# Rotary embedding on one core: four start-up requests on SyncE's queue (x row 0, sine, x row 1, cosine) in place of three (sine, x rows 0 and 1, cosine)

## The chip, the cores and the metric

One core of one Trainium2 chip runs the kernel. The metric is the device time of one execution in microseconds (us), the median of repeated runs. The kernel before took 316.51 us, the median of three runs between 316.38 and 316.61. A separate execution was recorded by the hardware profiler; all views and records quoted here are of that execution.

## What is computed

A rotary position embedding is applied to x of shape (8, 2048, 16, 64): batch, position, head, channel. Each position has a row of 32 cosines and 32 sines, which all batches and heads share.

```
x1 = x[..., :32]
x2 = x[..., 32:]
out1 = x1 * cos - x2 * sin
out2 = x1 * sin + x2 * cos
out = concatenate([out1, out2], axis=-1)
```

Input and output are float32, 67.1 MB each. The arithmetic is small beside moving that much in and out of HBM.

## The kernel before

**Layout.** The 2048 positions of a batch are laid over 128 partitions, 16 consecutive positions to a partition (J = 16). One "row" j of a partition is one position: 16 heads by 64 channels, 1024 values, 4 KB in float32. A batch is thus 128 partitions of 16 rows, 8.4 MB in HBM. In the core's memory x is kept as float16 in `buf`, which has five slots (NBUF = 5); batch b uses slot b mod 5. The transfers issued from GpSimd (POOL) convert between float32 in HBM and float16 in `buf` on their way.

**Start-up.** Transfers issued from SyncE (SP) do not convert. So the first two rows of batch 0 (JA = 2) are fetched by SP in float32 into a tile of their own, `head` (8 KB to a partition, 1 MB in all, lines 41 to 44). The sine table goes to `sin_f` (line 40) and the cosine table to `cos_f` (line 45), each 2 KB to a partition and 256 KB in all. SP issues these three at the start, and nothing else until the end of the kernel. ScalarE (ACT) then casts, in this order: sine to `sin_h` (line 104), minus sine to the other half of `sin_h` (line 105), `head` to rows 0 and 1 of `buf` slot 0 (line 106), cosine to `cos_h` (line 110).

**GpSimd's transfers.** All other loads and stores are issued by POOL, on one queue, in an order that `in_ring` fixes (loads at line 71, stores at line 81):

1. load of rows 2 to 15 of batch 0
2. load of batch 1
3. store of row 0 of batch 0
4. load of batches 2 and 3 as one transfer, then of batch 4
5. store of rows 1 to 15 of batch 0, stores of batches 1 and 2
6. load of batches 5 and 6 as one transfer, then of batch 7 (slots 0, 1 and 2 again)
7. store of batches 3 and 4, store of batches 5 and 6, two stores with rows 0 to 13 of batch 7

The third entry has to wait until the first two rows of batch 0 are finished, and the fourth is behind it in POOL's order.

**Compute.** `rotate(b, j0, j1)` is three VectorE (DVE) instructions: v = swapped halves of x times the signed sine (line 92), x = x times cosine (line 98), x = x + v (line 100). DVE runs rotate for rows 0 and 1 of batch 0, for rows 2 to 15 of batch 0, and then for batches 1 to 7. The first line 92 needs `sin_h` and the cast `head`; the first line 98 needs `cos_h` too.

**End.** The last two rows of batch 7 are cast back to float32 by ACT into `head` (line 134) and stored by SP (line 135), which waits until the store of rows 0 to 8 of batch 7 has landed.

Of the kernel before, what the change touches and what calls it, by code (L numbers as in the profile page):

```python
# [1 line left out]

# [4 lines left out]


@with_exitstack  # L10
def kernel(
    ctx: ExitStack,
    tc: tile.TileContext,
    x: bass.AP,
    cos: bass.AP,
    sin: bass.AP,
    out: bass.AP,
):
    nc = tc.nc
    f16 = mybir.dt.float16  # L20
    f32 = mybir.dt.float32

    B, S, H, D = x.shape
    Dh = D // 2
    P = nc.NUM_PARTITIONS
    J = S // P
    NBUF = 5

    const_pool = ctx.enter_context(tc.tile_pool(name="rope_const", bufs=1))
    io_pool = ctx.enter_context(tc.tile_pool(name="rope_io", bufs=1))  # L30
    tmp_pool = ctx.enter_context(tc.tile_pool(name="rope_tmp", bufs=1))

    JA = 2
    head = const_pool.tile([P, JA, H, D], f32)
    x0 = x[0].rearrange("(p j) h d -> p j (h d)", j=J)
    sin_f = const_pool.tile([P, J, Dh], f32)
    cos_f = const_pool.tile([P, J, Dh], f32)
    cos_h = const_pool.tile([P, J, Dh], f16)
    sin_h = const_pool.tile([P, J, D], f16)
    nc.sync.dma_start(out=sin_f, in_=sin.rearrange("(p j) d -> p j d", j=J))  # L40
    nc.sync.dma_start(  # L41
        out=head.rearrange("p j h d -> p (j h d)"),
        in_=x0[:, 0:JA, :].rearrange("p j f -> p (j f)"),
    )
    nc.sync.dma_start(out=cos_f, in_=cos.rearrange("(p j) d -> p j d", j=J))

    buf = io_pool.tile([P, NBUF, J, H, D], f16)

    ring = []

    def in_ring(dma):
        if ring:
            tc.add_manual_dep(
                dma.ins,
                ring[-1].ins.name,
                mybir.DependencyInfo(mybir.DependencyClass.NoSync, mybir.DependencyReason.DATA),
                reason="order of the ring",
            )
        ring.append(dma)
        return dma  # L60

    def load(b, n=1):
        k = b % NBUF
        if n == 1:
            j0 = JA if b == 0 else 0
            dst = buf[:, k, j0:J, :, :].rearrange("p j h d -> p (j h d)")
            src = x[b].rearrange("(p j) h d -> p j (h d)", j=J)[:, j0:J, :].rearrange("p j f -> p (j f)")
        else:
            dst = buf[:, k : k + n, :, :, :].rearrange("p b j h d -> p b (j h d)")
            src = x[b : b + n].rearrange("b (p j) h d -> p b (j h d)", j=J)  # L70
        in_ring(nc.gpsimd.dma_start(out=dst, in_=src))  # L71

    def store(b, n=1, j0=0, j1=J):
        k = b % NBUF
        if n == 1:
            src = buf[:, k, j0:j1, :, :].rearrange("p j h d -> p (j h d)")
            dst = out[b].rearrange("(p j) h d -> p j (h d)", j=J)[:, j0:j1, :].rearrange("p j f -> p (j f)")
        else:
            src = buf[:, k : k + n, :, :, :].rearrange("p b j h d -> p b (j h d)")
            dst = out[b : b + n].rearrange("b (p j) h d -> p b (j h d)", j=J)  # L80
        return in_ring(nc.gpsimd.dma_start(out=dst, in_=src))  # L81

    def rotate(b, j0=0, j1=J):
        v = tmp_pool.tile([P, J, H, D], f16)
        n = j1 - j0
        js = slice(j0, j1)
        xt = buf[:, b % NBUF, js, :, :]
        shape = [P, n, H, 2, Dh]
        sin_b = sin_h[:, js, :].rearrange("p j (e d) -> p j e d", e=2).unsqueeze(2).to_broadcast(shape)
        cos_b = cos_h[:, js, :].unsqueeze(2).to_broadcast([P, n, 2 * H, Dh])  # L90
        xe = xt.rearrange("p j h (e d) -> p j h e d", e=2)
        nc.vector.tensor_mul(  # L92
            out=v[:, js, :, :].rearrange("p j h (e d) -> p j h e d", e=2),
            in0=xe[:, :, :, ::-1, :],
            in1=sin_b,
        )
        xw = xt.rearrange("p j h (e d) -> p j (h e) d", d=Dh)
        nc.vector.tensor_mul(out=xw, in0=xw, in1=cos_b)  # L98
        xa = xt.rearrange("p j h d -> p (j h d)")
        nc.vector.tensor_add(out=xa, in0=xa, in1=v[:, js, :, :].rearrange("p j h d -> p (j h d)"))  # L100

    load(0)
    load(1)
    nc.scalar.copy(out=sin_h[:, :, Dh:D], in_=sin_f)  # L104
    nc.scalar.mul(out=sin_h[:, :, 0:Dh], in_=sin_f, mul=-1.0)  # L105
    nc.scalar.copy(  # L106
        out=buf[:, 0, 0:JA, :, :].rearrange("p j h d -> p (j h d)"),
        in_=head.rearrange("p j h d -> p (j h d)"),
    )
    nc.scalar.copy(out=cos_h, in_=cos_f)  # L110
    rotate(0, 0, JA)
    store(0, 1, 0, 1)
    load(2, 2)
    load(4)
    rotate(0, JA, J)
    store(0, 1, 1, J)
    rotate(1)
    store(1)
    rotate(2)
    store(2)  # L120
    load(5, 2)
    load(7)
    rotate(3)
    rotate(4)
    store(3, 2)
    rotate(5)
    rotate(6)
    store(5, 2)
    rotate(7)
    gate = store(7, 1, 0, 9)  # L130
    store(7, 1, 9, J - JA)
    last = buf[:, 7 % NBUF, J - JA : J, :, :].rearrange("p j h d -> p (j h d)")
    dst = out[B - 1].rearrange("(p j) h d -> p j (h d)", j=J)[:, J - JA : J, :].rearrange("p j f -> p (j f)")
    nc.scalar.copy(out=head.rearrange("p j h d -> p (j h d)"), in_=last)  # L134
    end = nc.sync.dma_start(out=dst, in_=head.rearrange("p j h d -> p (j h d)"))
    tc.add_manual_dep(
        end.ins,
        gate.ins.name,
        mybir.DependencyInfo(mybir.DependencyClass.Sync, mybir.DependencyReason.DATA),
        reason="the last rows go out behind this part",  # L140
    )


# [1 line left out]
_INS = ['x', 'cos', 'sin']  # L145
_OUTS = [((8, 2048, 16, 64), 'float32')]


# [23 lines left out]
```

## Time and profile before

| what | value |
|---|---|
| median of the runs | 316.51 us |
| profiled execution: span from first to last instruction | 314.8 us (314.836 in the trace) |
| median minus span (start and end of an execution, outside the span) | 1.7 us |
| DVE busy | 209.1 us, 66% of the span |
| ACT busy | 6.8 us |
| POOL busy | 8.6 us |
| mean traffic in HBM | 428 GB/s over the span |
| first SP request issued / first POOL request issued | 0.74 us / 1.24 us |
| sine, head, cosine: issue to landing | 2.7, 6.9, 24.4 us |

How to read it: an instruction that issues a transfer costs its engine half a microsecond or so; the transfer itself is carried by the core's 16 DMA engines, which serve the queues of SP and POOL together. The view of issues gives the time from the issue to the landing, which is when the instruction that waits may start. The trace also holds a record of every piece that a DMA engine moved, with its start, its duration, its size and its queue. For a load or a store of 128 partitions there are 128 such pieces, eight to each DMA engine, one partition's share each (below called a *piece*), and after them on each engine a 4-byte piece that signals completion (below called a *mark*). Sizes in these records are those at the destination. Their times are given here from the start of the span.

### The profile page before, as it was taken

To read this page: it belongs to the slowest core of one execution; us is meant where nothing else is said; L and a number is where in the kernel's file an instruction comes from. 1 tells how busy PE (TensorE), PEld (TensorE's weight loads), DVE (VectorE), ACT (ScalarE), POOL (GpSimd) and SP (SyncE) were. 2 spreads that over 40 slices of the span, in tenths; PEclk is the share of its full clock that TensorE was granted. 3 is DMA by queue.
4 is the path that set the end of the run, shared out by engine and by line. 5 is a ranking of instruction groups with operands and counts; after the bars stand their busy time and mean duration, and the time that the engine had idled before them with its cause. 6 is when DMAs were issued, how large, how long until landed. Compare 5 with 4: busy or idle time off the path is not lost.

```text
span 314.8 us, 115 instructions
## 1 busy us (share of the span) xinstructions
DVE 209.1 (66%) x27; ACT 6.8 (2%) x6; POOL 8.6 (3%) x18
## 2 busy tenths in 40 slices
DVE  0105999999499999999950000899999999910000
ACT  3200000000000000000000000000000000020000
POOL 1002000000000000000010000000000000010000
DMA  9899999999999899999999999999999999999998
GB/s 284 187 262 200 200 266 200 200 262 204 200 200 317 382 492 407 400 400 533 400 200 208 258 200 200 229 237 333 400 491 441 400 400 525 408 400 400 433 427 339
DMA packets 3104, 101.71 MB, mean 323 GB/s; under 512 B 288, under 2 KB 288, under 8 KB 672
## 3 DMA queue, kind: packets, MB, share of 16 engines
q0 software_dynamic: 2528, 99.09, 98.1%
q1 hardware_dynamic: 576, 2.62, 2.2%
HBM read 67.63 MB, written 67.11 MB: 428 GB/s over the span
## 4 chain that ended last, share of the span: by engine, by line
DVE 66%; another core or an unknown queue 13%; DMA 8%; ACT 1%; issue 0%; SPq 0%; DVEq 0%; ACTq 0%
DVE buf L98 22%; DVE buf L100 22%; DVE v L92 22%; DMA cos_f<-in_cos_dram 8%; ACT head L134 1%; ACT cos_h L110 0%; SPq L41 0%; SPq L40 0%; DVEq L92 0%; ACTq L134 0%
## 5 line engine op out<-in xcount | busy, mean ns | idle before, releaser
L92 DVE TENSOR_TENSOR v<-buf,sin_h 128x16384 f16<-128x16384 f16 (+2 forms) x9 | 69.7, 7744 | 51.4 <-DMA buf<-in_x_dram 41.2
L98 DVE TENSOR_TENSOR buf<-buf,cos_h 128x16384 f16<-128x16384 f16 (+2 forms) x9 | 69.7, 7744 | 15.8 <-ACT cos_h L110 15.5
L100 DVE TENSOR_TENSOR buf<-buf,v 128x16384 f16<-128x16384 f16 (+2 forms) x9 | 69.7, 7744 | 0.3
L81 POOL DMA_DIRECT2D out_dram<-buf x8 | 4.7, 586 | 219.4 <-DVE buf L100 219.4
L134 ACT CAST head<-buf 128x2048 f32<-128x2048 f16 x1 | 1.9, 1898 | 249.9 <-DVE buf L100 249.9
L71 POOL DMA_DIRECT2D buf<-in_x_dram x6 | 3.7, 628 | 49.7 <-DMA out_dram<-buf 48.9
L106 ACT CAST buf<-head 128x2048 f16<-128x2048 f32 x1 | 1.9, 1897 | 3.5 <-DMA head<-in_x_dram 3.5
L104 ACT ACT_TABLE_LOAD x1 | 1.3, 1283 | 0.7 <-PEq L156 0.7
L110 ACT CAST cos_h<-cos_f 128x512 f16<-128x512 f32 x1 | 0.6, 617 | 16.1 <-DMA cos_f<-in_cos_dram 16.1
L104 ACT CAST sin_h<-sin_f 128x512 f16<-128x512 f32 x1 | 0.6, 617 | 1.4 <-DMA sin_f<-in_sin_dram 1.4
L105 ACT ACTIVATE sin_h<-sin_f 128x512 f16<-128x512 f32 x1 | 0.6, 624 | 0.0
L156 POOL MEMSET const-float32-0.0<- 128x1 f32 x1 | 0.1, 100 | 0.2 <-issue 0.2
L156 POOL MEMSET const-bfloat16-1.0<- 128x1 bf16 x1 | 0.1, 103 | 0.0
L156 POOL MEMSET const-float32-1.0<- 128x1 f32 x1 | 0.1, 100 | 0.0
L156 POOL MEMSET const-uint8-127<- 128x1 uint8 x1 | 0.1, 100 | 0.0
## 6 DMA issues: line engine op xcount, KB each, us to landing
buf<-in_x_dram POOLq DMA_DIRECT2D x2, 8192.0 KB, 55.2
buf<-in_x_dram POOLq DMA_DIRECT2D x3, 4096.0 KB, 57.4
out_dram<-buf POOLq DMA_DIRECT2D x1, 7680.0 KB, 68.3
out_dram<-buf POOLq DMA_DIRECT2D x1, 4608.0 KB, 28.6
buf<-in_x_dram POOLq DMA_DIRECT2D x1, 3584.0 KB, 22.3
out_dram<-buf POOLq DMA_DIRECT2D x1, 2560.0 KB, 34.1
head<-in_x_dram SPq DMA_DIRECT2D x1, 1024.0 KB, 6.9
out_dram<-head SPq DMA_DIRECT2D x1, 1024.0 KB, 8.4
```

Source lines behind the costliest of these rows:

```text
L71: in_ring(nc.gpsimd.dma_start(out=dst, in_=src))
L81: return in_ring(nc.gpsimd.dma_start(out=dst, in_=src))
L92: nc.vector.tensor_mul(out=v[:, js, :, :].rearrange("p j h (e d) -> p j h e d", e=2), in0=xe[:, :, :, ::-1, :], in1=sin_b,)
L98: nc.vector.tensor_mul(out=xw, in0=xw, in1=cos_b)
L100: nc.vector.tensor_add(out=xa, in0=xa, in1=v[:, js, :, :].rearrange("p j h d -> p (j h d)"))
L104: nc.scalar.copy(out=sin_h[:, :, Dh:D], in_=sin_f)
L105: nc.scalar.mul(out=sin_h[:, :, 0:Dh], in_=sin_f, mul=-1.0)
L106: nc.scalar.copy(out=buf[:, 0, 0:JA, :, :].rearrange("p j h d -> p (j h d)"), in_=head.rearrange("p j h d -> p (j h d)"),)
L110: nc.scalar.copy(out=cos_h, in_=cos_f)
L134: nc.scalar.copy(out=head.rearrange("p j h d -> p (j h d)"), in_=last)
L156: nc = _bacc.Bacc("TRN2", target_bir_lowering=False, num_devices=1)
```

## The change

Only the start-up requests of SP change. The request for `head` is split by rows, its first half goes ahead of the sine table, its second half behind it. The cosine table stays last. Per partition the four requests carry 4 KB, 2 KB, 4 KB and 2 KB where the three carried 2 KB, 8 KB and 2 KB.

```
-    nc.sync.dma_start(out=sin_f, in_=sin.rearrange("(p j) d -> p j d", j=J))
-    nc.sync.dma_start(
-        out=head.rearrange("p j h d -> p (j h d)"),
-        in_=x0[:, 0:JA, :].rearrange("p j f -> p (j f)"),
-    )
+    nc.sync.dma_start(out=head[:, 0, :, :].rearrange("p h d -> p (h d)"), in_=x0[:, 0, :])
+    nc.sync.dma_start(out=sin_f, in_=sin.rearrange("(p j) d -> p j d", j=J))
+    nc.sync.dma_start(out=head[:, 1, :, :].rearrange("p h d -> p (h d)"), in_=x0[:, 1, :])
     nc.sync.dma_start(out=cos_f, in_=cos.rearrange("(p j) d -> p j d", j=J))
```

The instructions of DVE, ACT, POOL and TensorE are the same, in the same order; SP has one more issue. ACT's cast of `head` is still one instruction over both rows, so it waits for both halves. Lines behind the edit stand two lower in the changed kernel (line 98 becomes line 96).

## The prediction

> **What bounds the kernel now.** I read the page's head first, then the issues, the timeline of the first 60 us, the chain, and last the trace's records of single pieces.
>
> ```profile
> DVE 209.1 (66%) x27; ACT 6.8 (2%) x6; POOL 8.6 (3%) x18
> ...
> DMA  9899999999999899999999999999999999999998
> ...
> HBM read 67.63 MB, written 67.11 MB: 428 GB/s over the span
> ```
>
> DVE is busy for two thirds only, while the DMA row is full from the first slice to the last. The piece records say it more sharply: from 2.2 us to 310.7 us all 16 DMA engines serve one piece after the other without a gap. So the span is the DMA engines' work plus whatever time they stand still, and an edit costs time if it adds work to them or lets their queues run dry.
>
> ```profile
> buf<-in_x_dram POOLq DMA_DIRECT2D x1, 3584.0 KB, 22.3
> ...
> head<-in_x_dram SPq DMA_DIRECT2D x1, 1024.0 KB, 6.9
> ...
> out_dram<-buf POOLq DMA_DIRECT2D x1, 512.0 KB, 15.2
> sin_f<-in_sin_dram SPq DMA_DIRECT2D x1, 256.0 KB, 2.7
> cos_f<-in_cos_dram SPq DMA_DIRECT2D x1, 256.0 KB, 24.4
> ```
>
> The sine and the cosine table are equally large; one takes 2.7 us to land and the other 24.4. That is the row to explain. What follows from it is in the timeline:
>
> ```profile
> 1.24 1.21 POOL L71 DMA_DIRECT2D buf<-in_x_dram  x2 [0.80 <-PEq L167]
> 1.65 0.42 SPq L45 DMA_DIRECT2D cos_f<-in_cos_dram  x1
> ...
> 26.10 0.62 ACT L110 CAST cos_h<-cos_f 128x512 f16<-128x512 f32 x1 [16.09 <-DMA cos_f<-in_cos_dram]
> 26.75 1.23 DVE L98 TENSOR_TENSOR buf<-buf,cos_h 128x2048 f16<-128x2048 f16 x1 [15.48 <-ACT cos_h L110]
> ...
> 29.53 0.54 POOL L81 DMA_DIRECT2D out_dram<-buf  x1 [27.08 <-DVE buf L100]
> ```
>
> Until the cosine is there (26.08), DVE cannot finish rows 0 and 1, POOL cannot issue their store (29.53), and the loads of batches 2 to 4 stand behind that store. Meanwhile the DMA engines live on the two loads issued at 1.24. Their last mark is at 42.7 to 43.1 us in the piece records, and the store's pieces follow at once.
>
> **Why the cosine is late.** Each DMA engine carries 8 pieces and a mark of every request. From the records of one engine: sine pieces 0.084 us each, head pieces 0.309 us, first load 2.13 us, second load 2.43 us. Sine and head are served in one run from 1.8 to 5.3-5.6 us. Then come a piece of the load, the mark of head, a piece of the load, a cosine piece, a piece of the load, a cosine piece, and so on: cosine pieces begin at about 9.7, 11.8, 14, 16.2, 18.4, 20.6, 22.8 and 23.1 us, the marks at 25.4-25.7. So **one piece of SP's queue is served for each entry of POOL's queue.** Of SP's 27 entries, 17 or 18 went ahead and 9 or 10 were left to alternate; the tenth turn ends at 25.7, which gives the landing.
>
> The question that decides this case is what put the border behind the eighth head piece. All 16 engines have it there, though they reach it between 5.28 and 5.62 us, so a software load that became ready at one moment near 5.4 us would have found them at different pieces. The end of the kernel shows another mechanism.
>
> ```profile
> 305.57 0.35 SPq L135 DMA_DIRECT2D out_dram<-head  x1
> ```
>
> SP's first piece at the start began 1.03 us after its issue (0.74 to 1.77). Here it begins at 310.72, 5.2 us after the issue: on every engine five pieces of POOL's store that had not begun by 306.6 (0.79 us each) and its mark still go first. They were **already in a line of some six to eight entries** in front of each engine. A line of eight explains the start as well: sine was nearly through by 2.7-3.1 us, the line then held the eight head pieces, and the load, arriving near 3 us, queued behind them and took turns from there with what was still outside the line (mark, cosine). That puts the load's arrival 1.0 to 2.0 us after its issue at 1.24, where without a line it would be 4.04 us.
>
> **The change, part by part.** Instructions on DVE, ACT and POOL are the same.
>
> *Extra issue and pieces.* One more SP issue, 0.43 us by the rows of lines 41 and 45, delays the cosine's issue from 1.65 to about 2.1 us; SP has nothing behind it until 305 us. Eight 4 KB pieces twice in place of eight of 8 KB: no SP piece of 4 KB is shown; by the straight line through 0.084 (2 KB) and 0.309 (8 KB) it takes 0.159 us, so 8 x (2 x 0.159 - 0.309) plus a 0.01 us mark is +0.08 us (bounds 8 x (2 x 0.084 - 0.309) = -1.1 and 8 x 0.309 = +2.5 us; the line is nearest).
>
> *Order.* SP's queue on each engine becomes 8 row-0 pieces, mark, 8 sine, mark, 8 row-1, mark, 8 cosine, mark: 36 entries. First data again near 1.8 us. In before the first pieces lost 0.3 us on average; 8 x 0.16 us then puts the end of row 0 near 3.5 us, where before the sine ended at 2.7-3.1. At 3.0 us an engine has done four or five row-0 pieces; the line of eight holds the rest of row 0, its mark and three or four sine pieces. POOL's load enters there. Left to alternate are 4 or 5 sine pieces, a mark, and 9 entries each for row 1 and cosine: **23 or so where there were 10.** POOL has only 18 entries in its two loads (8 + mark, 8 + mark). So the last cosine pieces run out behind the end of both loads. By the rows, 8 x 2.13 + 8 x 2.43 us of load from about 3.9 us, with 18 small ones between (some 2.3 us), end near 42.7; five left-over pieces take 0.4. I expect the cosine at about 43.3 us, not 26.1; sine lands near 15 and row 1 near 35, both earlier than it.
>
> *What is late then.* The 17 us themselves are hidden or not by the DMA queue alone: it has work until 43. The chain behind the cosine is unchanged: 0.34 us from the mark to the landing, 3.45 us from the landing to POOL's store (26.08 to 29.53: cast, two DVE instructions, POOL's wake-up), and then from the issue to the first piece. That last term is not shown alone: 1.0 us by SP's row at the start, 4.04 us by the load's first piece (1.24 to 5.28); I take 1.8, nearest to the arrival worked out above. The engines stand still for 0.34 + 3.45 + 1.8 = 5.6 us (4.8 to 7.8).
>
> The Trainium skill, "DMA: Bandwidth & Descriptors", section "Specifications", gives a first-byte latency of about 1 us for this path; by that the pause would be 4.8 us.
>
> *Whether it is won back.* DVE starts 17 us later and ends batch 1 at 78.4 + 17.1 = 95.5. In before it then waited for the load of batches 2 and 3:
>
> ```profile
> 78.40 4.89 another core or an unknown queue
> ...
> 161.88 36.10 another core or an unknown queue
> ```
>
> That load lands at 83.3 + 5.6 = 88.9 now, so the first wait vanishes and DVE ends batch 4 at 174 (161.9 before); batches 5 and 6 land at 198 + 5.6 = 203.6. Every store is issued before the queue in front of it ends (first ones 69.7, 95.9 and 122 us against 108, 126 and 146). DVE's delay dies in the second wait, the queue is never dry again, and the 5.6 us stay. Sum: 5.6 + 0.08 = 5.7 us; span 314.8 to 320.5, and 316.51 + 5.7 = **322.2 us** on the median, which lies 1.7 us above the span.
>
> **Rivals.**
>
> *The border comes late (not slower).* The load becomes ready only near 5.3 us, as its first piece shows at face value, and there is no line. SP's first three requests end at 5.4-5.7 us, so one row-1 piece at most is left; the cosine lands at 26 to 28.5. DVE has 4.89 us to spare and the queue lasts to 43, so nothing is lost: 316.6 us. It decides for this if at most three row-1 entries alternate in addition (six or more begin to cost). For it: the load is first seen at 5.28. Against it: the wait of 5.2 us at the end, and the same border on 16 unequal engines. Chance 0.13, with the next sentences in it.
>
> The Trainium skill, same page, section "Queues, rings and completion order", says that an engine drains a whole packet, typically 9 to 17 descriptors, from one queue before it turns to the next. By that row 1 and cosine would cost one or two turns each, and the time would stay at 316.6; the trace shows eight cosine pieces in eight turns, which speaks against it.
>
> *Part of the way.* Row 1 is half in when the load arrives (after about 3.9 us): 14 to 17 entries left, the cosine between 35 and 43 us. With 16 left it lands one turn of 2.4 us before the queue ends: 5.7 - 2.4 = 3.3 us, 319.8. Chance 0.08.
>
> *Fuller start.* In before the first sine piece took up to 0.64 us and the first head piece up to 0.72, waiting for data; larger first pieces may close up to 0.7 us of that, with a late border: 315.8. Chance 0.03.
>
> **How the numbers follow.** Forecast 0.74, between 321.3 and 324.4 by the bounds of the pause; partial 0.08; not slower 0.13; faster 0.03; another 0.02 for a longer pause than any row shows. The range 317.2 to 324.5 takes the forecast and the partial case, 0.82. A measurement of this kernel tells about 0.2% (0.6 us) from no change: slower 0.84, same 0.13, faster 0.03.
>
> **What would show it.** The cosine's time to landing near 41 us, the sine's near 14; the DMA row with a hole in the slice around 43 to 49 us; POOL's first store near 46.7; only one wait of DVE for a load, near 30 us. It is wrong if sine still lands within 5 us, or if the cosine lands before 35.

## The result: 7.8 us slower

The changed kernel takes 324.30 us (five runs, 324.26 to 324.68) against 316.51 us (five runs, 316.38 to 316.67): ratio 1.0245, 95% interval 1.0234 to 1.0256. Its profiled span is 322.9 us against 314.8.

The head of its page, with the DMA row:

```profile
span 322.9 us, 119 instructions
...
DVE 209.1 (65%) x27; ACT 6.8 (2%) x6; POOL 8.6 (3%) x18
...
DMA  8999939999999999999999999999999999999997
...
HBM read 67.63 MB, written 67.11 MB: 417 GB/s over the span
```

All engines do the same work as before, and the same bytes move. New is the 3 in the sixth slice, 40.4 to 48.4 us: the DMA engines stand still for most of it. The issues (engine, KB, us to landing):

```profile
head<-in_x_dram SPq DMA_DIRECT2D x2, 512.0 KB, 13.2
...
out_dram<-buf POOLq DMA_DIRECT2D x1, 512.0 KB, 3.7
sin_f<-in_sin_dram SPq DMA_DIRECT2D x1, 256.0 KB, 4.2
cos_f<-in_cos_dram SPq DMA_DIRECT2D x1, 256.0 KB, 41.9
```

The cosine, still last in SP's queue, now needs 41.9 us instead of 24.4. The first store landed 15.2 us after its issue in the kernel before, since it waited behind loads; now it lands after 3.7, because nothing is in front of it. The timeline of the changed kernel shows the chain between the two:

```profile
5.41 0.62 ACT L102 CAST sin_h<-sin_f 128x512 f16<-128x512 f32 x1 [3.39 <-DMA sin_f<-in_sin_dram]
5.93 0.62 ACT L103 ACTIVATE sin_h<-sin_f 128x512 f16<-128x512 f32 x1
24.02 1.90 ACT L104 CAST buf<-head 128x2048 f16<-128x2048 f32 x1 [17.46 <-DMA head<-in_x_dram]
...
44.05 0.62 ACT L108 CAST cos_h<-cos_f 128x512 f16<-128x512 f32 x1 [18.14 <-DMA cos_f<-in_cos_dram]
44.70 1.23 DVE L96 TENSOR_TENSOR buf<-buf,cos_h 128x2048 f16<-128x2048 f16 x1 [17.53 <-ACT cos_h L108]
...
47.48 0.54 POOL L79 DMA_DIRECT2D out_dram<-buf  x1 [45.03 <-DVE buf L98]
```

The sine lands early, row 1 at 24 us (the cast of `head` waits for it), the cosine at 44, and POOL's store goes out at 47.48. The windows view, first of the kernel before, then of the changed one, over the same stretch (columns: stretch, its length, busy time of DVE, ACT and POOL with the number of instructions, clock, DMA share, GB/s; a piece is counted whole where it begins, so that a share can exceed 1):

```profile
43.60:48.50 4.90, 4.87 (x2) 0.00 (x0) 0.00 (x0) 1.00 1.11 251
```

```profile
43.60:48.50 4.90, 3.73 (x3) 0.62 (x1) 1.02 (x2) 1.00 0.00 0
```

No piece begins for 4.9 us, where before the engines were full. This standstill is called the **hole** below. By the piece records each engine stands still for 5.6 us on average between 40 and 60 us (their last marks are at 42.96 to 43.52, the store's first piece at 48.58).

DVE waits less, not more, later on. Its waits in the changed kernel:

```profile
DVE v L90 <- DMA buf<-in_x_dram: 31.3, 1, 31.3
...
DVE buf L96 <- ACT cos_h L108: 17.5, 1, 17.5
```

Before, it waited twice for a load, 4.9 and 36.1 us; now once.

### The profile page after: what moved, and what is told of

It is laid out like the page before. It is cut to its first block, busy times and chain, and to the rows that moved or that the text cites. A ratio compares the mean times of both kernels' runs of the same rounds, so it can differ in the third digit from the quotient of the medians.

```text
span 322.9 us, 119 instructions
## 1 busy us (share of the span) xinstructions
DVE 209.1 (65%) x27; ACT 6.8 (2%) x6; POOL 8.6 (3%) x18
## 4 chain that ended last, share of the span: by engine, by line
DVE 64%; DMA 13%; another core or an unknown queue 10%; ACT 1%; SPq 0%; issue 0%; ACTq 0%; DVEq 0%
DVE buf L96 22%; DVE buf L98 22%; DVE v L90 21%; DMA cos_f<-in_cos_dram 13%; ACT head L132 1%; ACT cos_h L108 0%; SPq L41 0%; SPq L42 0%; SPq L40 0%; ACTq L132 0%; DVEq L90 0%
## 5 line engine op out<-in xcount | busy, mean ns | idle before, releaser
L90 DVE TENSOR_TENSOR v<-buf,sin_h 128x16384 f16<-128x16384 f16 (+2 forms) x9 | 69.7, 7744 | 57.5 <-DMA buf<-in_x_dram 31.3
```

What stands on the lines that cost most here:

```text
L90: nc.vector.tensor_mul(out=v[:, js, :, :].rearrange("p j h (e d) -> p j h e d", e=2), in0=xe[:, :, :, ::-1, :], in1=sin_b,)
```

## The experiments

Three questions: is it the order of the requests or their number; is it the hole or DVE's late start; what sets the border between the pieces that go ahead and those that take turns. Diffs are against the changed kernel unless said otherwise. "Excess" is the median minus the median of the kernel before on the same chip (316.5 to 316.7).

### e1: the sine first, then row 0, row 1, cosine

```
-    nc.sync.dma_start(out=head[:, 0, ...], in_=x0[:, 0, :])
     nc.sync.dma_start(out=sin_f, ...)
+    nc.sync.dma_start(out=head[:, 0, ...], in_=x0[:, 0, :])
     nc.sync.dma_start(out=head[:, 1, ...], in_=x0[:, 1, :])
     nc.sync.dma_start(out=cos_f, ...)
```

> Four requests as in the change, but the sine first: sine, row 0, row 1, cosine. Theory A (border by arrival: POOL's load gets in behind SP's second request, what SP asked for later takes turns with it, and the engines' queue runs dry): row 1 and cosine behind the border, 18 entries, cosine lands near 42 us after its issue, 323 to 325 us. Theory B (putting row 0 ahead of the sine is what costs): as before, 316.5 us. Theory C (the border is set by when SP's work ends, about 5.4 us): cosine at 26 to 28 us, 316.6 us.

324.22 us, ratio 1.0241 (1.0226 to 1.0256). The cosine needs 42.0 us, the hole is 5.7 us. Theory A holds; putting x ahead of the sine (B) is not the cause, and C falls.

### e2: three requests, both rows ahead of the sine (against the kernel before)

```
+    nc.sync.dma_start(out=head..., in_=x0[:, 0:JA, :]...)
     nc.sync.dma_start(out=sin_f, ...)
-    nc.sync.dma_start(out=head..., in_=x0[:, 0:JA, :]...)
     nc.sync.dma_start(out=cos_f, ...)
```

> Three requests as before, but both rows in one request ahead of the sine: rows 0 and 1, sine, cosine. Theory A: two requests are in before POOL's load, only the cosine takes turns, lands near 24 us after its issue as before, 316.5 us (316.2 to 316.9). Theory B (x ahead of the sine costs): about 324 us. Theory of a line of eight pieces: the line holds rows, so the sine's nine entries and the cosine's nine take turns, cosine near 42, about 324 us.

317.01 us, ratio 1.0011 (1.0002 to 1.0021): 0.1 us above A's range, and not by A's route. Its issues:

```profile
sin_f<-in_sin_dram SPq DMA_DIRECT2D x1, 256.0 KB, 13.4
cos_f<-in_cos_dram SPq DMA_DIRECT2D x1, 256.0 KB, 31.8
```

The border lies inside the sine: by the records some 6 of its 8 pieces to an engine go ahead, 2 and the mark take turns, and so the cosine is 7 us later than before. The store still reaches the engines before their loads end (its first piece at 42.78 us, no hole), which is why 7 us cost next to nothing. The line of eight, by which the prediction counted, falls: 15 entries or so went ahead here, and about 12 of them had not begun at 3.1 us, by when the load can have reached an engine (e3).

### e3: a tiny request first (against the kernel before)

```
+    tiny = const_pool.tile([1, Dh], f32)
+    nc.sync.dma_start(out=tiny, in_=sin[0:1, :])
     nc.sync.dma_start(out=sin_f, ...)
```

> The kernel before with one more SP request ahead of its three: 128 bytes of the sine table to one partition, a result that nothing reads. It adds one SP issue of about 0.4 us and next to no work. Theory A: every SP request is issued 0.4 us later against POOL's load, so head falls behind the border with the cosine, 18 entries, cosine near 42 us after its issue, 322 to 325 us. A theory by which the split of head or its number of pieces costs: as before, 316.6 us. Border at the end of SP's work: 316.6 us.

323.88 us, ratio 1.0226 (1.0209 to 1.0243). 128 bytes nobody needs cost 7.2 us, because every request behind them is issued 0.4 us later against POOL's load:

```profile
0.74 0.34 SPq L41 DMA_DIRECT2D tiny<-in_sin_dram  x1
1.13 0.36 SPq L42 DMA_DIRECT2D sin_f<-in_sin_dram  x1
1.24 1.21 POOL L73 DMA_DIRECT2D buf<-in_x_dram  x2 [0.80 <-PEq L169]
1.54 0.42 SPq L43 DMA_DIRECT2D head<-in_x_dram  x1
```

The load's first piece starts at 3.10 us, 1.86 after its issue, where the kernel before has 5.28: so the load can be at an engine that early. It is no more than an upper bound for this engine, since the piece follows at once on the mark of the sine. One engine had no work from 3.47 us on, and its first piece of the load came at 4.04, 2.8 us after the issue; in e8 three idle engines waited for it until 3.6 to 4.5 us after. So the load does not reach all engines at one time.

In the kernel before, the changed one, e1 and e3 the SP request issued 0.07 to 0.11 us before POOL's load goes ahead of it, and the one issued 0.30 to 0.41 us after it takes turns. That the border is set by the time of arrival is argued, not shown. It does not follow from the first pieces alone: SP's first request begins 1.03 us after its issue, and at that rate row 1 (issued at 1.64) would be there by 2.7 us, ahead of the load. SP's third request must take longer: the idle engine of e3 had no piece of `head`, issued at 1.54, by 4.04. Why was not tried.

### e4: a load ahead of the store

```
-    store(0, 1, 0, 1)
     load(2, 2)
+    store(0, 1, 0, 1)
     load(4)
```

> The changed kernel with POOL issuing the load of batches 2 and 3 ahead of the store of row 0, so that the engines have work while the cosine is late. Theory A (the loss is the dry queue): cosine still near 42 us after its issue, DVE still starts 18 us late, but no hole, 316.4 to 317.3 us. Rival D (the loss is DVE's late start): about 324 us.

317.56 us, ratio 1.0034 (1.0021 to 1.0047); 0.3 us above A's range, far from D's 324. The timeline shows that nothing else was mended:

```profile
44.61 0.62 ACT L108 CAST cos_h<-cos_f 128x512 f16<-128x512 f32 x1 [18.15 <-DMA cos_f<-in_cos_dram]
...
48.04 0.57 POOL L79 DMA_DIRECT2D out_dram<-buf  x1 [44.89 <-DVE buf L98]
```

The cosine and DVE are as late as in the changed kernel, yet 6.7 of the 7.8 us are back. It is the hole that costs, not DVE's start. 0.9 us remain without any hole; by the records SP's pieces take 0.6 us more on each engine than in the kernel before, and the engines stand still 0.7 us longer at the two ends, while POOL's pieces take 0.3 less.

### e5 and e6: POOL's first load later

```
+    spare = buf[:, 4, :, :, :].rearrange("p j h d -> p (j h d)")
+    nc.gpsimd.memset(spare[:, 0:512], 0.0)      (e6: 0:1536)
     load(0)
```

> The changed kernel with one more POOL instruction, a fill of 128x512 values in a free slot, ahead of its first load, so that the loads come some 0.5 us later while SP's four requests keep their times. Theory A (border by arrival): row 1 comes ahead of the border if the delay is 0.4 us or more, the cosine alone takes turns and lands near 26 us, no hole, 316.5 to 317.3 us. Theory E (the four requests cost by themselves, whenever POOL's load comes): about 324 us.

324.59 us, ratio 1.0246 (1.0229 to 1.0263). It tells nothing of the two theories: the fill ran from 0.74 to 1.26 us, in time that POOL spends waiting in the other kernels, and the load went out at 1.27 instead of 1.25. It is the changed kernel once more.

> The same with a fill three times as long (128x1536), a delay of 1 to 2 us. Theory A: all four requests are in before the load, cosine lands near 6 us, DVE starts near 10 us instead of 44, and the time is still only 316.3 to 317.5 us, since the engines were busy all along in the kernel before as well; it is up to 1 us more if the load comes after SP's pieces are through. Theory E: about 324 us. A theory by which an early DVE start is worth something in itself: below 316.

317.53 us, ratio 1.0036 (1.0019 to 1.0052). Here the load moved by 0.8 us:

```profile
1.63 0.42 SPq L42 DMA_DIRECT2D head<-in_x_dram  x1
2.06 1.21 POOL L69 DMA_DIRECT2D buf<-in_x_dram  x2
2.09 0.43 SPq L43 DMA_DIRECT2D cos_f<-in_cos_dram  x1
...
24.98 0.62 ACT L110 CAST cos_h<-cos_f 128x512 f16<-128x512 f32 x1 [15.73 <-DMA cos_f<-in_cos_dram]
```

Row 1, issued 0.43 us before the load, went ahead, so it is not only SP's first two requests that can. Of the cosine, issued 0.04 us after the load, about half of the pieces went ahead; the rest took turns, and it lands at 25, near the 26 of the kernel before (I had it at 6 us). No hole, and the loss shrinks to 0.9 us with all four requests and their pieces in place: theory E falls. Two of the ten runs were longer, 319.90 and 323.07 us; why is not known.

### e7 and e8: fewer pieces in the third request

```
-    nc.sync.dma_start(out=head[:, 0, ...], in_=x0[:, 0, :])
+    flat = head.rearrange("p j h d -> p (j h d)")
+    rows = x0[:, 0:JA, :].rearrange("p j f -> p (j f)")
+    nc.sync.dma_start(out=flat[0:64, :], in_=rows[0:64, :])      (e8: 0:32)
     nc.sync.dma_start(out=sin_f, ...)
-    nc.sync.dma_start(out=head[:, 1, ...], in_=x0[:, 1, :])
+    nc.sync.dma_start(out=flat[64:P, :], in_=rows[64:P, :])      (e8: 32:P)
```

> The order of the change, but head is split by partitions instead of rows: both rows of partitions 0 to 63, sine, both rows of partitions 64 to 127, cosine. The third request has four pieces to an engine instead of eight, 14 entries are behind the border instead of 18. Theory A with one turn for each entry: cosine lands four turns of 2.5 us after the 26.1 us of before, near 36 us; POOL's store then reaches the engines near 40.5 us, ahead of the end of the loads at 43, no hole, 316.5 to 317.4 us. If the turn goes by requests or bytes, not by pieces: cosine near 43, about 324 us.

> The same with 32 partitions in the first request and 96 in the third: six pieces to an engine, 16 entries behind the border. Theory A: cosine lands near 41 us, the store's first piece near 45.6, a hole of about 2.6 us in place of 5.5; 319.2 to 321.5 us, depending on how much of the 2 us that the changed kernel loses beside its hole comes with any hole. Theory by which the loss is all or nothing (by the number of requests): 324 us or 316.6.

323.04 us, ratio 1.0200 (1.0169 to 1.0230), and 323.79 us, 1.0224 (1.0209 to 1.0239): both expectations missed. The four runs of e7 spread from 321.94 to 324.00, and its profile is of the longest. There SP's issues became slower:

```profile
0.74 0.55 SPq L42 DMA_DIRECT2D head<-in_x_dram  x1
1.25 1.21 POOL L71 DMA_DIRECT2D buf<-in_x_dram  x2 [0.80 <-PEq L167]
1.35 0.56 SPq L43 DMA_DIRECT2D sin_f<-in_sin_dram  x1
```

The sine is issued 0.10 us after the load now, and its last piece or its mark takes turns too: one turn more than I counted on three engines, two on twelve, three on the last one. The sine's marks show it, at 7.5 us on the three, 9.4 to 9.9 on the twelve and 11.58 on the last; the cosine's marks follow the same steps, at 38.8, near 41.2 and at 43.46, and the landing waits for the last. So within e7 one entry costs one turn. In e8 the cosine's marks come at 40.7 to 41.3 us on nine engines and at 42.5 to 43.4 on seven; four of its engines had stood still from 4.15 us, until their next piece came at 4.89 to 5.79. The landing is late as soon as one engine is, and so the two kernels neither prove nor deny that the loss goes by turns.

### e9 and e10: a shorter hole

```
+    load_rows(2, 0, 2)      (e10: four rows)
     store(0, 1, 0, 1)
-    load(2, 2)
+    load_rows(2, 2, J)
+    load(3)
     load(4)
```

> The changed kernel with two of the sixteen rows of batch 2 loaded ahead of the store of row 0 (the rest of batch 2, batch 3 and batch 4 behind it, as three loads). It gives the engines 1.05 MB more, 2.5 us, before they run dry, and nothing else. Theory A: cosine at 44 us and the store's first piece near 48.6 us as in the changed kernel, hole 5.5 - 2.5 = 3.0 us; 319.5 us if the loss is the hole alone, up to 321.8 us if the 2.2 us beside the hole in the changed kernel come with any hole. Rival D (DVE's late start costs): 324 us.

> The same with four rows of batch 2, 2.1 MB or 4.9 us of work ahead of the store. Theory A: hole 5.5 - 4.9 = 0.6 us, 317.1 us from the hole alone, up to 319.3 us if a restart costs whatever the length of the hole. Rival D: 324 us.

322.42 us, ratio 1.0189 (1.0172 to 1.0206), and 319.82 us, 1.0102 (1.0087 to 1.0117). Both lie 0.5 to 0.6 us above A's ranges; the holes are 3.5 and 1.0 us by the records, not 3.0 and 0.6. D falls with e10, while e9 alone would not decide. The windows view of e9, then of e10:

```profile
44.00:48.00 4.00, 2.61 (x3) 0.62 (x1) 0.00 (x0) 1.00 0.44 89
48.00:49.00 1.00, 1.00 (x1) 0.00 (x0) 0.90 (x2) 1.00 0.00 0
```

```profile
44.00:48.00 4.00, 2.92 (x3) 0.62 (x1) 0.21 (x1) 1.00 0.97 203
48.00:49.00 1.00, 1.00 (x1) 0.00 (x0) 1.00 (x3) 1.00 0.18 57
```

The excess follows the hole with the same rest on top: 5.9 us for 3.5, 3.3 for 1.0, and 7.8 for 5.6 in the changed kernel. So a part of the loss does not shrink with the hole.

### e11: row 1 last

```
-    nc.sync.dma_start(out=head[:, 1, ...], in_=x0[:, 1, :])
     nc.sync.dma_start(out=cos_f, ...)
+    nc.sync.dma_start(out=head[:, 1, ...], in_=x0[:, 1, :])
```

> The changed kernel with its last two requests exchanged: row 0, sine, cosine, row 1. Theory A: again 18 entries behind the border, now row 1 is the last to land, near 43.6 to 44 us, the cosine near 24. Behind row 1 stand ACT's cast of both rows (1.90 us) and three DVE instructions instead of ACT's cast of the cosine (0.62) and two: the hole is 1.3 + 1.3 = 2.5 us longer, 326.3 to 327.3 us. A theory by which it is the cosine's lateness that costs: about 317 us.

327.25 us, ratio 1.0334 (1.0318 to 1.0349), as expected. The cosine lands after 22.1 us, earlier than in the kernel before, and this is the slowest kernel of all. What counts is the last request behind the border and the chain behind it:

```profile
44.49 1.90 ACT L104 CAST buf<-head 128x2048 f16<-128x2048 f32 x1 [37.41 <-DMA head<-in_x_dram]
...
50.53 0.54 POOL L79 DMA_DIRECT2D out_dram<-buf  x1 [48.08 <-DVE buf L98]
```

The store goes out at 50.53 instead of 47.48, the hole is 8.9 us instead of 5.6, the median 2.95 us longer.

### e12: all four requests ahead of the load

The edit of e6 with a fill of 3072 values; the load is issued at 3.34 us.

> The changed kernel with a fill of 128x3072 values on POOL ahead of its first load, which then is issued near 3.4 us instead of 1.25, when all four of SP's requests are out. Theory A: all four land by 7 or 8 us, DVE starts rows 0 and 1 near 10 us, 34 us earlier than in the changed kernel and 16 us earlier than before; the time is that of before plus what the engines stand still at the start, 316.5 to 318.5 us. A theory by which an early start of DVE brings something: below 316.

317.49 us, ratio 1.0030 (1.0018 to 1.0042). All four have landed by 7.6 us:

```profile
cos_f<-in_cos_dram SPq DMA_DIRECT2D x1, 256.0 KB, 5.5
```

DVE starts at 9.0 us and is through with rows 0 and 1 at 12.8, 16 us before the kernel before. It then waits for the loads that much longer, and nothing is gained. No kernel tried is faster than the kernel before.

## Why the prediction was right, and where its steps were not

- **What bounds the kernel: right.** The DMA engines' work and their standing still make the time. e4 and e12 show it from both sides: a late DVE start costs at most 0.9 us without a hole, an early one brings nothing.
- **One entry of SP for one of POOL: right.** With 18 entries behind the border, and POOL's two loads holding 18, the cosine's marks are at 43 us with the end of the second load. Predicted landing 43.3, measured 44.03.
- **The line of eight: wrong.** By it part of the sine and 23 entries should have been behind the border, sine near 15 us, row 1 near 35. The sine landed by 5.41, 4.2 us after its issue, and row 1 at 24.0: one of the two signs that I had named for being wrong did come. The border lies behind the request that was issued just before POOL's load, in the changed kernel as in the kernel before. No fixed length of a line gives it: 14 or so entries that had not begun at 3.1 us went ahead in the changed kernel, seven or eight in the kernel before. A request issued close to the load can be cut in two (e2, e6, e7). What sets the border is open. The error did not change the forecast, since 18 entries and 23 both outlast the 18 of POOL; that is luck, since a border one request later would have left 9, as in the kernel before, which has no hole.
- **The pause: right in size, by errors that cancel.** Predicted 5.6 us, measured 5.6. Its parts: 0.34 from the last mark to the landing was 0.5; 3.45 to POOL's store was 3.45; 1.8 to the first piece was 1.10 (47.48 to 48.58); the rest is that most engines end before the last. The Trainium skill, "DMA: Bandwidth & Descriptors", section "Specifications", has about 1 us for this first byte: the trace agrees here (1.10).
- **Nothing is won back: right.** Batch 1 ended at 96.4 on DVE (95.5 predicted), batch 4 at 174.9 (174); one wait of 31.3 (near 30).
- **The sum stopped at the hole: this was the term mis-sized.** Forecast 5.7, measured 7.8 (8.05 on the span). Beside the hole of 5.58 the records show three things that I had at 0.08 in all. SP's start-up pieces take 0.46 us more on each engine: a 4 KB piece costs 0.209 us on average, not 0.159. POOL's pieces take 310.41 us on each engine instead of 308.98, 1.43 more, most of it in slow pieces: the first one on each engine of the load behind the hole takes about 3.2 us instead of 2.43, and the last one of batch 4's load, just ahead of the next store, 3.3. And the engines stand still 0.53 us longer at the two ends. 5.58 + 0.46 + 1.43 + 0.53 is 8.00 of the 8.05.
- **The range: met by luck.** 324.30 lies 0.2 us inside the upper end, 324.5. That end stood for a pause of 7.8 us, and the pause was 5.6; the terms left out of the sum filled the rest.
- **How sure is that rest?** The excess minus the hole is 1.5 to 2.5 us in all nine kernels with a hole, with holes from 1.0 to 8.9 us, and 0.9 in e4, e6 and e12, which have the split and no hole (each also moves a request of POOL, so the split's own share was not isolated). The records part the two: POOL's pieces take 309.9 to 310.8 us on each engine in the nine kernels with a hole, and 308.7 to 309.0 in the five without. So a hole came with 1.0 to 1.9 us of slower pieces, 1.0 with the longest hole (e11) and 1.4 with the shortest (e10). Why those pieces are slow was not tested.
- **The rivals.** The late border fell with e3, where the load's first piece starts at 3.10 us. Part of the way did not come: all 18 entries were left. Nor did the fuller start: the engines stand still 0.2 us longer at the start. Typically 9 to 17 descriptors in one turn, the rule of the Trainium skill, "DMA: Bandwidth & Descriptors", section "Queues, rings and completion order", fell in the prediction's reading of it, one descriptor to a piece, with the cosine's 41.9 us: its eight pieces took eight turns.

## What to carry to other kernels

When all DMA engines are busy throughout, look for the point at which their queue could run dry, and ask which landing has to come before it; lateness up to that point is free, and beyond it each microsecond counts, here with one to two more for slow pieces after the restart. A small request that is issued a fraction of a microsecond after a large one shares the engines with it piece by piece, and may land only when the large one ends. So count requests and their times of issue, not bytes: what the first work needs goes out first, and as few requests as possible ahead of the large stream.

## What the runs showed of the hardware that I had not expected

- 128 bytes requested first cost 7.2 us (e3), because the 0.4 us that they add to SP's issue put 1 MB on the other side of the border.
- The time from POOL's issue to the first piece was no constant: 4.04 us for the load of the kernel before, behind SP's pieces; at most 1.86 on the first engine of e3; 2.8 to 4.5 on engines that stood idle waiting for it (e3, e8); and 1.10 for the store after the hole.
- In e7 each of SP's four start-up issues took 0.49 to 0.63 us, those over 128 partitions like those over 64; in the changed kernel they took 0.38 to 0.43. Why is open.
